# Feed-forward block sums of a hybrid diffusion step: made from kept full-precision blocks and rebuilt blocks, with no GpSimd instruction

## The chip, the core and the metric

The kernel runs on one core of a Trainium2 chip. The metric is the device time of one execution, in microseconds (us). TensorE (PE) multiplies, VectorE (DVE), ScalarE (ACT) and GpSimd (POOL) do the elementwise work, and each of them executes its own instruction stream in order. SyncE issues the weight transfers.

## The reference

Two layers run over 640 tokens (128 of a context, 512 of a latent grid) of width 1024. Each layer is a half-step SwiGLU feed-forward, a token mixer (attention in layer 0, a long convolution in layer 1), and a second feed-forward. Every sub-layer reads a modulated input and ends in a layer norm:

```
def modulate(x, shift, scale):
    return x * (1.0 + scale) + shift

def swiglu(h, w_in, w_out):
    g, u = jnp.split(h @ w_in, 2, axis=-1)
    return (jax.nn.silu(g) * u) @ w_out

x = layer_norm(ALPHA * x + 0.5 * g1 * swiglu(modulate(x, sh1, sc1), ffn_w_in_i[0], ffn_w_out_i[0]), ...)
mix, extras = mixer(modulate(x, sh2, sc2))
x = layer_norm(ALPHA * x + g2 * mix, ...)
x = layer_norm(ALPHA * x + 0.5 * g3 * swiglu(modulate(x, sh3, sc3), ffn_w_in_i[1], ffn_w_out_i[1]), ...)
```

The width of `w_in` is 2 x 2816, so each of the four feed-forwards has 22 hidden tiles of 128.

## The kernel before

Activations are stored transposed: `x[:, dt, token]` holds feature tile `dt` (0 to 7) for all 640 tokens, which fall into two halves of 320, `c = 0` and `c = 1`. Half 0 holds both kinds of tokens (128 and 192), which have different modulation vectors, so an ACT instruction that modulates a tile of half 0 is issued as two (128 and 192 columns) and one of half 1 as a single one (320 columns).

Every fp32 product is made of three reduced-precision ones: an operand is split in a high half (`xh`, `wh`, `hh`; a cast on ACT, line 157) and a low half (`xl`, `wl`, `hl`; a subtraction on DVE, line 158), and three matmuls per 128 x 128 block (lines 516 to 518) add up.

A feed-forward stage (`ffn`, `idx` 0 to 3) starts with two or three "plain" hidden tiles (`do_plain`: both gate and up product for each token half, eight feature tiles each) and makes the others "fast" (`do_fast`): a two by two block scheme with seven products of four feature tiles in place of eight. It needs sums of weight blocks, which GpSimd makes (`s1` to `s4`, lines 593 to 596, two buffers), and three sums of activation blocks, made once in each stage: with the blocks x11, x21 (half 0, feature tiles 0 to 3 and 4 to 7) and x12, x22 (half 1), T1 = x12 - x11, T2 = x22 - T1, T4 = x21 - T2, and a further one, T2 - x11, which replaces x12 in `xh` and `xl` after the plain tiles are through (`combine_rest`). `combine_blocks` makes them from the split halves `xh`, `xl` that exist already: five DVE subtractions and additions and two splits for each of four tiles, and four GpSimd instructions (lines 543 to 546), on tiles named `ta` and `tb`; the splits go to tiles named `t`.

Ahead of that stands the layer norm of half 1 (`norm_steps`), which runs beside the first plain products: when its scale `rs` is there, DVE multiplies each `x` tile by it (line 425), ACT modulates it into a temporary `xm` (line 362), and `modulate_out` splits it into `xh`, `xl`. `rescale` then turns the normalised `x` itself into its scaled form, in place, on GpSimd (line 466, 16 tiles in a stage); in program order it stands between the fast tiles. Temporaries of `tmp` share a ring of six buffers.

A plain tile's two products sit in two of five accumulator banks. The gate's bank comes free when ACT has made its Silu (line 585, tile `sg`), the up product's when DVE has multiplied it in (line 573). The order in which each engine's instructions stand is chosen at build time by a scheduler, within the dependencies; it is not written by hand.

Of the kernel before, what the change touches and what calls it, by code (L numbers as in the profile page):

```python
# [12 lines left out]
F32 = mybir.dt.float32  # L13
F32R = mybir.dt.float32r
AF = mybir.ActivationFunctionType
ALU = mybir.AluOpType
# [9 lines left out]
CH = T // 2  # L26
# [52 lines left out]
T1, T2, T4 = (0, 1), (2, 3), (4, 5)  # L79
# [5 lines left out]
def kernel(  # L85
# [5 lines left out]
    te, act, dve, pool, sp = nc.tensor, nc.scalar, nc.vector, nc.gpsimd, nc.sync  # L91
# [21 lines left out]
    def tmp(name, cols=T, parts=P, dt=F32):  # L113
        t = tp.tile([P, UW], F32, tag="t", name=name)
        return t[:parts, :cols]
# [40 lines left out]
    def split(pair, src, eng=None):  # L156
        act.copy(pair[0], src)  # L157
        (eng or dve).tensor_tensor(pair[1], src, pair[0], ALU.subtract)  # L158
# [154 lines left out]
    xh = res.tile([P, KD, T], F32R, name="xh")  # L313
    xl = res.tile([P, KD, T], F32R, name="xl")
    fill = []
    tt = []
# [19 lines left out]
    CSL = (slice(0, CH), slice(CH, T))  # L336
# [22 lines left out]
    def mod_apply(dst, dt, c, st):  # L359
        for sl, z in SEG[c]:  # L360
            o = slice(sl.start - CSL[c].start, sl.stop - CSL[c].start)
            act.activation(dst[:, o], x[:, dt, sl], AF.Identity, bias=drv[:, st, 1, dt, z:z + 1],
                           scale=drv[:, st, 0, dt, z:z + 1])

    def modulate(dt, c, st):
        modulate_out(dt, c, modulate_in(dt, c, st))

    def modulate_in(dt, c, st):
        xm = tmp(f"xm{st}_{dt}_{c}", CH)
        mod_apply(xm, dt, c, st)  # L370
        return xm

    def modulate_out(dt, c, xm):
        if dt in XDVE[c]:
            dve.tensor_copy(xh[:, dt, CSL[c]], xm)
        else:
            act.copy(xh[:, dt, CSL[c]], xm)
        eng = pool if dt in XPOOL[c] else dve
        eng.tensor_tensor(xl[:, dt, CSL[c]], xm, xh[:, dt, CSL[c]], ALU.subtract)  # L379
# [7 lines left out]
    def norm_steps(c, st, bank, nsum):  # L387
# [35 lines left out]
        for dt in range(KD + (LAG if st < 5 else 0)):  # L423
            if dt < KD:
                ins = dve.tensor_tensor(x[:, dt, sl], x[:, dt, sl], rs, ALU.mult)
                if dt > LAG:
                    pin(ins)
            if st < 5:
                if dt < KD:
                    xms.append(modulate_in(dt, c, st + 1))  # L430
                if dt >= LAG:
                    modulate_out(dt - LAG, c, xms[dt - LAG])
            else:
                act.activation(x[:, dt, sl], x[:, dt, sl], AF.Identity, bias=lnb[:, st, dt:dt + 1],
                               scale=lng[:, st, dt:dt + 1])
                sp.dma_start(out=a["y"][:, dt, sl], in_=x[:, dt, sl])
# [82 lines left out]
            if n == KD and i % 4 == 3:  # L519
                tick()  # L520

    def pair_tmp(name):
        t = tmp(name, 2 * CH)
        return t[:, 0:CH], t[:, CH:2 * CH]

    def xf(dt, c):
        return [t[:, dt, CSL[c]].bitcast(F32) for t in (xh, xl)]

    def combine_blocks(st):
        pairs = [pair_tmp(f"ta{st}_{k}") for k in range(4)]  # L530
        for k, (t1, t2) in enumerate(pairs):
            u = tmp(f"tb{st}_{k}", CH)
            (h11, l11), (h12, l12), (h22, l22) = xf(k, 0), xf(k, 1), xf(k + 4, 1)
            dve.tensor_tensor(t1, h12, h11, ALU.subtract)
            dve.tensor_tensor(u, l12, l11, ALU.subtract)
            dve.tensor_tensor(t1, t1, u, ALU.add)
            dve.tensor_tensor(t2, h22, t1, ALU.subtract)
            dve.tensor_tensor(t2, t2, l22, ALU.add)
            for src, (h, l) in ((t2, T2), (t1, T1)):
                split((tt[h][:, k], tt[l][:, k]), src)  # L540
        for k, (t1, t2) in enumerate(pairs):
            (h11, l11), (h21, l21) = xf(k, 0), xf(k + 4, 0)
            pool.tensor_tensor(t1, h21, t2, ALU.subtract)
            pool.tensor_tensor(t1, t1, l21, ALU.add)
            pool.tensor_tensor(t2, t2, h11, ALU.subtract)
            pool.tensor_tensor(t2, t2, l11, ALU.subtract)
        return pairs

    def combine_rest(pairs):
        for k, (t4, t3) in enumerate(pairs):  # L550
            split((xh[:, k, CSL[1]], xl[:, k, CSL[1]]), t3)
        for k, (t4, t3) in enumerate(pairs):
            split((tt[T4[0]][:, k], tt[T4[1]][:, k]), t4)

    def ffn(l, j, hp, fbank, following):
        idx = 2 * l + (0 if j == 0 else 1)
# [10 lines left out]
        for g0, g1 in GROUPS:  # L567
# [20 lines left out]
            def do_fast(f):  # L588
# [8 lines left out]
                for u, src in ((u11, a11), (u2, s2), (u1, s1), (u12, a12), (u3, s3), (u4, s4), (u22, a22)):  # L597
                    split(u, src)
                b1, b2, b3 = [fbank(f"f{idx}_{f}_{i}") for i in range(3)]
                p1, p5 = pair_tmp(f"p{idx}_{f}")  # L600
                q, u3_ = pair_tmp(f"q{idx}_{f}")
                sg0, sg1 = pair_tmp(f"sg{idx}_{f}")
                product(b1, [u11], 0, xb(range(4), 0))
# [18 lines left out]
            if g0 == 0:  # L622
                for f, c in [(0, 0), (1, 0), (0, 1), (1, 1)] + [(f, c) for f in range(2, NPLAIN[idx]) for c in range(2)]:
                    if (f, c) == (0, 1):
                        settle()
                        t3 = combine_blocks(st)
                    do_plain(f, c)
                combine_rest(t3)
# [417 lines left out]
    def filters(consts):  # L1046
# [8 lines left out]
        with tc.tile_pool(name="fl", bufs=1) as fl, tc.tile_pool(name="fps", bufs=3, space=PSUM) as fps, \  # L1055
# [163 lines left out]
            for it in range(8):  # L1219
                if it == XLOAD:  # L1220
                    del raws[NRAW:]
                    sp.dma_start(out=x, in_=a["xT"])
                if it == XLOAD + 1:
                    for dt in range(KD):
                        modulate(dt, 0, 0)
                gen = spectrum(it)
                for i in range(5):
                    next(gen)
                    if it + 1 < 8:
                        taps(it + 1, i)  # L1230
                    if i < SFILL[1 + it]:
                        fill_step()
                if it + 2 < 8:
                    prepare(it + 2)
# [314 lines left out]
    with es:  # L1549
        for dt in range(KD):  # L1550
            modulate(dt, 1, 0)
        ffn(0, 0, hp, fbank, [("wv", 0, 0), ("wv", 0, 1), ("wqk", 0, 0)])
# [178 lines left out]
```

## Time and profile before

| | |
|---|---|
| time, median of three runs | 2839.18 us (2838.5 to 2842.29) |
| the profiled execution's own time | 2846.74 us |
| its span, first to last instruction | 2845.0 us |
| mean granted TensorE clock, of full speed | 0.977 |
| busy: PE, DVE, ACT, POOL | 95%, 76%, 41%, 38% |

The profile is of one execution; its instructions and waits add up to the span, and some 2 us of the execution lie outside it. The median is of other executions. An engine's share is a mean over stages that have different limits.

### The profile page before, as it was taken

What the parts mean: (1) busy time and instruction counts of PE and PEld (TensorE: products, weight loads), DVE (VectorE), ACT (ScalarE), POOL (GpSimd) and SP (SyncE); (2) the same over time, 40 slices, a digit from 0 to 9 for tenths busy, and PEclk for the clock granted to TensorE, in tenths of its full rate; (3) what the DMA queues carried; (4) which work ended last, traced back from release to release, by engine and by line L of the source; (5) the groups of instructions that cost most, each with busy time, mean ns of one, the idle gap of its engine ahead of it and who ended that gap; (6) DMA issues with size and microseconds to landing.
All of it is one profiled execution on the core that took longest, in us unless ns stands there. A gap on an engine that the chain in (4) does not pass through costs nothing.

```text
span 2845.0 us, 51146 instructions
## 1 busy us (share of the span) xinstructions
PE 2702.4 (95%) x19404; PEld 2574.7 (90%) x19404; DVE 2157.5 (76%) x4778; ACT 1174.0 (41%) x2508; POOL 1067.2 (38%) x891
## 2 busy tenths in 40 slices
PE   7988999999999988999998999999999988999998
PEld 6888999989999678999988999998999987999997
DVE  6697889865665688888979888886777777865764
ACT  5642433444444353434345243344333335433433
POOL 4462543440000163534445354344223235643542
PEclk9999999999999989999999999998999999999999
DMA  8623333313222523243231433332423331212311
GB/s 289 223 69 113 118 99 119 113 54 95 76 72 73 192 68 119 90 127 123 86 105 38 130 112 108 119 111 73 130 78 109 101 97 41 90 61 89 97 62 59
DMA packets 111135, 293.46 MB, mean 103 GB/s; under 512 B 13823, under 2 KB 28927, under 8 KB 110760
## 3 DMA queue, kind: packets, MB, share of 16 engines
q1 hardware_dynamic: 107576, 285.80, 31.4%
q0 software_dynamic: 2304, 4.20, 0.5%
q8 instruction: 153, 2.51, 0.4%
q14 instruction: 94, 0.77, 0.1%
q10 hardware_dynamic: 1008, 0.19, 0.1%
HBM read 275.98 MB, written 14.16 MB: 102 GB/s over the span
## 4 chain that ended last, share of the span: by engine, by line
PE 62%; DVE 21%; DMA 6%; issue 4%; POOL 4%; ACT 3%; DVEq 0%; SPq 0%; POOLq 0%; ACTq 0%
PE f L516 6%; PE f L517 6%; PE f L518 6%; PE o L516 5%; PE o L517 5%; PE o L518 5%; DVE junk L247 4%; DVE wl L158 4%; DMA mh<-in_modt 3%; DVE xl L158 2%; PE hy L343 2%; PE hy L342 2%; PE hy L344 2%; POOL s L595 2%; POOL s L596 2%
## 5 line engine op out<-in xcount | busy, mean ns | idle before, releaser
L157 ACT CAST wh<-raw 128x512 fp32r<-128x512 f32 (+1 forms) x327 | 230.3, 709 | 302.5 <-PE o L517 150.7
L158 DVE TENSOR_TENSOR wl<-raw,wh 128x512 fp32r<-128x512 f32 (+1 forms) x274 | 280.5, 1025 | 72.3 <-ACT wh L157 71.3
L516 PE MATMUL f<-xh,wh 128*128 128x320 f32 x956 | 302.3, 319 | 25.6 <-DVE q L606 13.5
L517 PE MATMUL f<-xl,wh 128*128 128x320 f32 x956 | 301.6, 316 | 3.2 <-DVE xl L379 3.1
L518 PE MATMUL f<-xh,wl 128*128 128x320 f32 x956 | 298.1, 314 | 0.0
L247 DVE SCALAR_TENSOR_TENSOR junk<-mh,condw 128x256 f32<-128x256 f32 x576 | 267.4, 511 | 34.1 <-DMA mh<-in_modt 33.8
L516 PE MATMUL o<-hh,wh 128*128 128x320 f32 x840 | 260.7, 314 | 5.2 <-ACT hh L157 5.2
L517 PE MATMUL o<-hl,wh 128*128 128x320 f32 x840 | 259.0, 309 | 0.0
L518 PE MATMUL o<-hh,wl 128*128 128x320 f32 x840 | 258.1, 309 | 0.0
L353 DVE SCALAR_TENSOR_TENSOR x<-o,drv,x 128x320 f32<-128x320 f32 (+2 forms) x384 | 153.8, 434 | 102.6 <-PE o L518 102.2
L158 DVE TENSOR_TENSOR wl<-s,wh 128x512 fp32r<-128x512 f32 x187 | 172.4, 922 | 72.0 <-ACT wh L157 68.5
L157 ACT CAST wh<-s 128x512 fp32r<-128x512 f32 x187 | 115.7, 620 | 242.6 <-POOL s L594 73.7
L516 PEld LDWEIGHTS f<-xh,wh 128*128 128x128 f32 x956 | 183.8, 193 | 31.8 <-DVE q L606 16.0
L516 PE MATMUL f<-xh,xh 128*128 128x320 f32 x628 | 196.6, 315 | 11.7 <-DVE q L606 5.3
L595 POOL TENSOR_TENSOR s<-raw,raw 128x512 f32<-128x512 f32 x77 | 115.9, 1506 | 238.1 <-DVE wl L158 149.9
L593 POOL TENSOR_TENSOR s<-raw 128x512 f32<-128x512 f32 x77 | 110.7, 1437 | 248.7 <-DVE junk L247 167.5
L517 PE MATMUL f<-xl,xh 128*128 128x320 f32 x628 | 195.5, 312 | 0.2 <-DVE xl L379 0.2
L518 PE MATMUL f<-xh,xl 128*128 128x320 f32 x628 | 193.8, 311 | 0.0
L517 PEld LDWEIGHTS f<-xl,wh 128*128 128x128 f32 x956 | 184.5, 193 | 6.1 <-DVE xl L379 5.8
L518 PEld LDWEIGHTS f<-xh,wl 128*128 128x128 f32 x956 | 183.8, 193 | 0.0
L516 PE MATMUL o<-hh,xh 128*128 128x320 f32 x568 | 177.7, 315 | 3.6 <-ACT hh L157 3.6
L517 PE MATMUL f<-t,wh 128*128 128x320 f32 x560 | 173.6, 311 | 4.1 <-DVE t L158 4.1
(490 smaller groups left out, 8975.5 us busy)
## 6 DMA issues: line engine op xcount, KB each, us to landing
raw<-in_win SPq DMA_DIRECT2D x176, 512.0 KB, 3.6
raw<-in_wout SPq DMA_DIRECT2D x88, 512.0 KB, 4.3
mh<-in_modt SPq DMA_DIRECT2D x144, 256.0 KB, 2.9
raw<-in_modw SPq DMA_DIRECT2D x62, 512.0 KB, 4.9
raw<-in_hyin SPq DMA_DIRECT2D x24, 512.0 KB, 4.0
ksb<-kspec SPq DMA_DIRECT2D x40, 256.0 KB, 2.7
kspec<-ks SPq DMA_DIRECT2D x32, 256.0 KB, 3.2
raw<-in_wqk SPq DMA_DIRECT2D x16, 512.0 KB, 3.7
```

Source lines behind the costliest of these rows:

```text
L157: act.copy(pair[0], src)
L158: (eng or dve).tensor_tensor(pair[1], src, pair[0], ALU.subtract)
L247: dve.scalar_tensor_tensor(junk, raw[:, 256 * g:256 * g + 256], 1.0, condw[0][:, z], ALU.mult, ALU.mult, accum_out=acc[:, g0 + g, t, z:z + 1])
L342: te.matmul(ps, wh[:, i, cols], kh(k), start=(i == 0), stop=False)
L343: te.matmul(ps, wh[:, i, cols], kl(k), start=False, stop=False)
L344: te.matmul(ps, wl[:, i, cols], kh(k), start=False, stop=(i == n - 1))
L353: dve.scalar_tensor_tensor(x[:, dt, sl], ps[:, o], drv[:, st, 2, dt, z:z + 1], x[:, dt, sl], ALU.mult, ALU.add)
L516: te.matmul(ps, wh, kh, start=(first and i == 0), stop=False, skip_group_check=True)
L517: te.matmul(ps, wh, kl, start=False, stop=False, skip_group_check=True)
L518: te.matmul(ps, wl, kh, start=False, stop=(last and i == n - 1), skip_group_check=True)
L593: pool.tensor_tensor(s1, a21, a22, ALU.add)
L595: pool.tensor_tensor(s3, a11, a21, ALU.subtract)
```

## The change

`modulate_in` keeps the full-precision modulated tiles of half 1 in feed-forward stages: two of them share one buffer of the ring (`kept_xm`, tiles `xk`), so that four buffers hold all eight. `combine_blocks` takes x12 and x22 from there, and rebuilds x11 and x21 by modulating `x` of half 0 again with ScalarE (tile `tb`, two tiles of two instructions each). The sums are made from these with four DVE subtractions and three splits for each of four tiles, and none on GpSimd. The fourth sum is written into buffers of kept tiles that are no longer needed, so that two of the four buffers come free. `rescale` of half 0 may no longer overwrite `x` before the rebuilding has read it.

```
@@ modulate_in
+    kept_xm = {}
+
+    def pair_tmp(name):
+        t = tmp(name, 2 * CH)
+        return t[:, 0:CH], t[:, CH:2 * CH]
...
     def modulate_in(dt, c, st):
-        xm = tmp(f"xm{st}_{dt}_{c}", CH)
+        if c == 1 and st % 3 != 1:
+            if dt < 4:
+                kept_xm[dt] = pair_tmp(f"xk{st}_{dt}")
+            xm = kept_xm[dt % 4][dt // 4]
+        else:
+            xm = tmp(f"xm{st}_{dt}_{c}", CH)
         mod_apply(xm, dt, c, st)
         return xm
@@ combine_blocks, combine_rest
     def combine_blocks(st):
-        pairs = [pair_tmp(f"ta{st}_{k}") for k in range(4)]
+        pairs, thirds = [kept_xm.pop(k) for k in range(4)], []
         for k, (t1, t2) in enumerate(pairs):
-            u = tmp(f"tb{st}_{k}", CH)
-            (h11, l11), (h12, l12), (h22, l22) = xf(k, 0), xf(k, 1), xf(k + 4, 1)
-            dve.tensor_tensor(t1, h12, h11, ALU.subtract)
-            dve.tensor_tensor(u, l12, l11, ALU.subtract)
-            dve.tensor_tensor(t1, t1, u, ALU.add)
-            dve.tensor_tensor(t2, h22, t1, ALU.subtract)
-            dve.tensor_tensor(t2, t2, l22, ALU.add)
-            for src, (h, l) in ((t2, T2), (t1, T1)):
-                split((tt[h][:, k], tt[l][:, k]), src)
-        for k, (t1, t2) in enumerate(pairs):
-            (h11, l11), (h21, l21) = xf(k, 0), xf(k + 4, 0)
-            pool.tensor_tensor(t1, h21, t2, ALU.subtract)
-            pool.tensor_tensor(t1, t1, l21, ALU.add)
-            pool.tensor_tensor(t2, t2, h11, ALU.subtract)
-            pool.tensor_tensor(t2, t2, l11, ALU.subtract)
-        return pairs
-
-    def combine_rest(pairs):
-        for k, (t4, t3) in enumerate(pairs):
+            x11, x21 = pair_tmp(f"tb{st}_{k}")
+            mod_apply(x11, k, 0, st)
+            mod_apply(x21, k + 4, 0, st)
+            dve.tensor_tensor(t1, t1, x11, ALU.subtract)
+            dve.tensor_tensor(t2, t2, t1, ALU.subtract)
+            split((tt[T2[0]][:, k], tt[T2[1]][:, k]), t2)
+            split((tt[T1[0]][:, k], tt[T1[1]][:, k]), t1)
+            dve.tensor_tensor(x21, x21, t2, ALU.subtract)
+            t3 = pairs[k - k % 2][1 - k % 2]
+            dve.tensor_tensor(t3, t2, x11, ALU.subtract)
+            thirds.append(t3)
+            split((tt[T4[0]][:, k], tt[T4[1]][:, k]), x21)
+        return thirds
+
+    def combine_rest(thirds):
+        for k, t3 in enumerate(thirds):
             split((xh[:, k, CSL[1]], xl[:, k, CSL[1]]), t3)
-        for k, (t4, t3) in enumerate(pairs):
-            split((tt[T4[0]][:, k], tt[T4[1]][:, k]), t4)
```

The scheduler's order moves with it, in much the same way in the second, third and fourth feed-forward. Three places of the second one follow (lines behind the edit are numbered one less, those between the two edits 11 more). First GpSimd, from the layer norm's subtractions (`x<-x,mus`) to the sums of the second fast tile. Before:

```order
L466 TENSOR_SCALAR x<-x,lng,lnb 128x320 x6
L400 TENSOR_TENSOR x<-x,mus_1_11626 128x320 x3
L466 TENSOR_SCALAR x<-x,lng,lnb 128x320 x8
L595 TENSOR_TENSOR s_3_2_12144<-raw_98,raw_99 128x512
L543 TENSOR_TENSOR ta_0_11834<-xh,ta_0_11834 128x320
L544 TENSOR_TENSOR ta_0_11834<-ta_0_11834,xl 128x320
L596 TENSOR_TENSOR s_3_3_12145<-raw_98,s_3_1_12143 128x512
L545 TENSOR_TENSOR ta_0_11834<-ta_0_11834,xh 128x320
L546 TENSOR_TENSOR ta_0_11834<-ta_0_11834,xl 128x320
L593 TENSOR_TENSOR s_4_0_12277<-raw_101 128x512
```

And now:

```order
L411 TENSOR_TENSOR x<-x,mus_1_11614 128x320 x3
L477 TENSOR_SCALAR x<-x,lng,lnb 128x320 x12
L594 TENSOR_TENSOR s_3_2_12120<-raw_98,raw_99 128x512
L477 TENSOR_SCALAR x<-x,lng,lnb 128x320
L595 TENSOR_TENSOR s_3_3_12121<-raw_98,s_3_1_12119 128x512
L477 TENSOR_SCALAR x<-x,lng,lnb 128x320 x3
L592 TENSOR_TENSOR s_4_0_12253<-raw_101 128x512
```

The `ta` instructions are gone, all rescales stand behind the layer norm's subtractions, and the weight sum `s_3_2` stands behind twelve of them.

Second ScalarE, from the cast of that weight sum (`wh_104<-s_3_2`) to the Silu of the first plain tile of half 1 (`sg_0_1`). Before:

```order
L157 CAST wh_104<-s_3_2_12144 128x512
L157 CAST xh_1_11262<-raw_101 128x512
L157 CAST xh_1_11266<-s_3_1_12143 128x512
L157 CAST t_1_11276<-ta_0_11834 128x320
L157 CAST wh_102<-raw_98 128x512
L157 CAST t_1_11274<-ta_1_11835 128x320
L157 CAST t_1_11274<-ta_2_11836 128x320
L585 ACTIVATE sg_0_1_11944<-f_0_1_0_11894 128x320
```

And now:

```order
L157 CAST wh_104<-s_3_2_12120 128x512
L362 ACTIVATE tb_2_11848<-x,drv 128x128
L362 ACTIVATE tb_2_11848<-x,drv 128x192
L362 ACTIVATE tb_2_11848<-x,drv 128x128
L362 ACTIVATE tb_2_11848<-x,drv 128x192
L362 ACTIVATE tb_3_11863<-x,drv 128x128
L362 ACTIVATE tb_3_11863<-x,drv 128x192
L362 ACTIVATE tb_3_11863<-x,drv 128x128
L362 ACTIVATE tb_3_11863<-x,drv 128x192
L157 CAST t_1_11262<-xk_2_11754 128x320
L157 CAST xh_1_11250<-raw_101 128x512
L584 ACTIVATE sg_0_1_11928<-f_0_1_0_11878 128x320
```

Between that cast and the Silu stand the eight instructions that rebuild the third and fourth pair of blocks, where three casts of sums and three of weights stood.

Third VectorE, around the split of the last feature tile of half 1 (`xl<-xm_7_1`, now the upper half of the kept buffer `xk_3`). Before:

```order
L379 TENSOR_TENSOR xl<-xm_6_1_11786,xh 128x320
L534 TENSOR_TENSOR ta_1_11835<-xh 128x320
L573 TENSOR_TENSOR sg_1_0_11829<-sg_1_0_11829,f_1_0_1_11804 128x320
L379 TENSOR_TENSOR xl<-xm_7_1_11791,xh 128x320
L537 TENSOR_TENSOR ta_0_11834<-xh,ta_0_11834 128x320
L535 TENSOR_TENSOR tb_1_11848<-xl 128x320
```

And now:

```order
L545 TENSOR_TENSOR xk_0_11748<-xk_1_11751,tb_1_11833 128x320
L158 TENSOR_TENSOR xl_1_11253<-raw_98,xh_1_11252 128x512
L158 TENSOR_TENSOR wl_103<-s_3_0_12118,wh_102 128x512
L158 TENSOR_TENSOR t_1_11265<-xk_0_11748,t_1_11264 128x320
L158 TENSOR_TENSOR t_1_11263<-xk_1_11751,t_1_11262 128x320
L158 TENSOR_TENSOR t_1_11267<-tb_0_11818,t_1_11266 128x320
L158 TENSOR_TENSOR t_1_11265<-xk_1_11751,t_1_11264 128x320
L158 TENSOR_TENSOR t_1_11267<-tb_1_11833,t_1_11266 128x320
L545 TENSOR_TENSOR xk_0_11748<-xk_0_11748,tb_0_11818 128x320
L390 TENSOR_TENSOR xl<-xk_3_11759,xh 128x320
```

The sums of the first two pairs are now complete ahead of that split. From the first multiplication by `rs` up to it there are 37 VectorE instructions, where there were 25; from the start of the stage to the last split of a sum there are four fewer. TensorE does the same 144 matmuls between `rs` and the third plain tile's second product as before; those that need the last feature tile of half 1 now stand last among them.

## Rows read from the trace of the kernel before

**Rows 1.** The page: busy time of each engine.

```profile
PE 2702.4 (95%) x19404; PEld 2574.7 (90%) x19404; DVE 2157.5 (76%) x4778; ACT 1174.0 (41%) x2508; POOL 1067.2 (38%) x891
```

**Rows 2.** Busy us (instructions) of PE, PEld, DVE, ACT, POOL; clock; DMA: four stretches.

```profile
129.00:187.00 58.00, 50.65 (x327) 49.81 (x326) 52.49 (x79) 31.30 (x66) 34.57 (x26) 0.94 0.21 64
1024.00:1091.00 67.00, 58.80 (x368) 57.59 (x367) 62.30 (x97) 34.15 (x73) 43.91 (x35) 0.92 0.13 40
1501.00:1592.00 91.00, 80.69 (x510) 79.15 (x510) 86.43 (x160) 43.32 (x91) 52.06 (x43) 0.94 0.28 85
2391.00:2450.00 59.00, 51.79 (x324) 50.33 (x323) 55.39 (x86) 29.37 (x63) 39.29 (x33) 0.94 0.14 45
```

**Rows 3.** PE's waits over the whole span: us in total, times, longest.

```profile
PE f L517 <- DVE t L158: 13.7, 5, 5.4
PE f L516 <- DVE sg L573: 9.4, 3, 4.2
...
PE f L516 <- ACT sg L585: 1.7, 2, 0.9
```

**Rows 4.** PE's waits for `q` in the second, third and fourth stretch of rows 2.

```profile
PE f L516 <- DVE q L606: 2.7, 1, 2.7
...
PE f L516 <- DVE q L606: 2.9, 2, 1.9
...
PE f L516 <- DVE q L606: 1.0, 1, 1.0
```

**Rows 5.** POOL's groups: one of four `ta` lines (1000 to 1090 us); weight sum (page).

```profile
L544 POOL TENSOR_TENSOR ta<-ta,xl 128x320 f32<-128x320 f32 x4 | 4.8, 1190 | 0.1
...
L595 POOL TENSOR_TENSOR s<-raw,raw 128x512 f32<-128x512 f32 x77 | 115.9, 1506 | 238.1 <-DVE wl L158 149.9 <-DVE xl L158 87.7
```

**Rows 6.** DVE in order of time, second feed-forward: start, us, line, operation.

```profile
1024.77 1.28 DVE L425 TENSOR_TENSOR x<-x,rs 128x320 f32<-128x320 f32 x3
...
1029.06 0.72 DVE L379 TENSOR_TENSOR xl<-xm,xh 128x320 fp32r<-128x320 f32 x1
...
1036.48 0.48 DVE L379 TENSOR_TENSOR xl<-xm,xh 128x320 fp32r<-128x320 f32 x1
...
1053.93 0.47 DVE L573 TENSOR_TENSOR sg<-sg,f 128x320 f32<-128x320 f32 x1
...
1056.81 1.15 DVE L537 TENSOR_TENSOR ta<-xh,ta 128x320 f32<-128x320 f32 x1
```

**Rows 7.** POOL in order of time, the same feed-forward.

```profile
1028.83 0.61 POOL L466 TENSOR_SCALAR x<-x,lng,lnb 128x320 f32<-128x320 f32 x1 [0.67 <-ACT xm L362]
...
1038.52 4.23 POOL L595 TENSOR_TENSOR s<-raw,raw 128x512 f32<-128x512 f32 x1 [3.10 <-DVE wl L158]
...
1056.50 1.11 POOL L544 TENSOR_TENSOR ta<-ta,xl 128x320 f32<-128x320 f32 x1
```

**Rows 8.** DVE's largest group of `combine`, 1020 to 1080 us.

```profile
L158 DVE TENSOR_TENSOR t<-ta,t 128x320 fp32r<-128x320 f32 x12 | 10.9, 908 | 0.0
```

**Rows 9.** ACT's groups by shape, 1000 to 1090 us.

```profile
L362 ACT ACTIVATE xm<-x,drv 128x192 f32<-128x192 f32 x8 | 4.3, 532 | 0.0
L362 ACT ACTIVATE xm<-x,drv 128x128 f32<-128x128 f32 x8 | 3.9, 487 | 4.3 <-DVE x L425 4.3
```

**Rows 10.** ACT in order of time, the same feed-forward.

```profile
1009.58 1.75 ACT L362 ACTIVATE xm<-x,drv 128x128 f32<-128x128 f32 x4 [1.23 <-DVE x L425]
...
1042.78 0.62 ACT L157 CAST wh<-s 128x512 fp32r<-128x512 f32 x1 [5.72 <-POOL s L595]
...
1045.95 0.43 ACT L585 ACTIVATE sg<-f 128x320 f32<-128x320 f32 x1
```

**Rows 11.** PE in order of time, the same feed-forward.

```profile
1024.14 0.56 PE L516 MATMUL f<-xh,wh 128*128 128x320 f32 x1
...
1045.35 0.31 PE L518 MATMUL f<-xh,wl 128*128 128x320 f32 x1
1046.43 0.42 PE L516 MATMUL f<-xh,xh 128*128 128x320 f32 x1 [0.77 <-ACT sg L585]
```

More of the change, by code (lines that the diff above doesn't have):

```diff
@@ L520, in product @@
                 tick()
[L522 to L527, printed above, removed]
     def combine_blocks(st):
-        pairs = [pair_tmp(f"ta{st}_{k}") for k in range(4)]
+        pairs, thirds = [kept_xm.pop(k) for k in range(4)], []
         for k, (t1, t2) in enumerate(pairs):
-            u = tmp(f"tb{st}_{k}", CH)
-            (h11, l11), (h12, l12), (h22, l22) = xf(k, 0), xf(k, 1), xf(k + 4, 1)
-            dve.tensor_tensor(t1, h12, h11, ALU.subtract)
-            dve.tensor_tensor(u, l12, l11, ALU.subtract)
-            dve.tensor_tensor(t1, t1, u, ALU.add)
-            dve.tensor_tensor(t2, h22, t1, ALU.subtract)
-            dve.tensor_tensor(t2, t2, l22, ALU.add)
-            for src, (h, l) in ((t2, T2), (t1, T1)):
-                split((tt[h][:, k], tt[l][:, k]), src)
-        for k, (t1, t2) in enumerate(pairs):
-            (h11, l11), (h21, l21) = xf(k, 0), xf(k + 4, 0)
-            pool.tensor_tensor(t1, h21, t2, ALU.subtract)
-            pool.tensor_tensor(t1, t1, l21, ALU.add)
-            pool.tensor_tensor(t2, t2, h11, ALU.subtract)
-            pool.tensor_tensor(t2, t2, l11, ALU.subtract)
-        return pairs
-    def combine_rest(pairs):
-        for k, (t4, t3) in enumerate(pairs):
+            x11, x21 = pair_tmp(f"tb{st}_{k}")
[13 more added lines that the diff above has]
+        for k, t3 in enumerate(thirds):
             split((xh[:, k, CSL[1]], xl[:, k, CSL[1]]), t3)
-        for k, (t4, t3) in enumerate(pairs):
-            split((tt[T4[0]][:, k], tt[T4[1]][:, k]), t4)
     def ffn(l, j, hp, fbank, following):
```

## The prediction

> **What bounds the kernel now.** I read the page first. TensorE is busy 95% of the span [rows 1], so what can be won without fewer matmuls is the time in which it waits, or runs at the lower of its two clocks. Then I looked for the four places at which the edited code works, one in each feed-forward, and asked for busy time and clock there [rows 2]. Two things are to be seen. VectorE, 76% busy over the span, is busy for 52.5 of 58, 62.3 of 67, 86.4 of 91 and 55.4 of 59 us: here it has almost no slack, while ScalarE is about half busy. And the mean granted clock is 0.92 to 0.94, where 1 is 2.4 GHz and 0.5 is 1.2 GHz: half-rate stretches cost 0.06 x 58 + 0.08 x 67 + 0.06 x 91 + 0.06 x 59 = 17.9 us.
>
> The list of waits says what TensorE waits for. For the low half of an activation sum (`t`): 13.7 us in 5 waits; for the multiplication behind Silu, which frees a plain tile's accumulator bank: 9.4 us in 3; for the Silu of such a tile: 1.7 us in 2 [rows 3]. These arise in the four places alone. For `q`, the first VectorE instruction on a fast tile's products, it waits in many places; in the three later ones it is 2.7 + 2.9 + 1.0 = 6.6 us [rows 4]. Together 31.4 us idle and 17.9 us of clock, 49.3 us: more than that the change can't win. The clock costs 17.9 / 31.4 = 0.57 us per idle us here, and I use that ratio below for idle time added or removed.
>
> **Removed.** Sixteen GpSimd instructions in each feed-forward, of about 1.15 us each (1.19 in one of the four groups [rows 5], 1.11 for one of them [rows 7]), some 18 us. GpSimd itself does not bound anything: it is busy 34.6 of 58 us and less than three quarters in all four places [rows 2]. What matters is what they do to VectorE. A subtraction of 320 columns takes 0.48 us alone (1036.48) and 1.15 us (1056.81) beside such an instruction, which ran from 1056.50 to 1057.61 [rows 6, 7]. The twelve low halves of sums in the second feed-forward took 0.908 us on average [rows 8]: 12 x 0.43 = 5.1 us lost in this group alone. If every one of the sixteen delayed one VectorE instruction by 0.67 us, it would be 10.7 us in a feed-forward. The relief is between 5.1 and 10.7 us, and I take 9, near the upper end, since the group of rows 8 is a third of the edited VectorE work and bears about half. Besides, four VectorE instructions fewer are issued in each feed-forward, at 0.40 us from start to start (three in 1.28 us, 1024.77 [rows 6]): 1.6 us. So VectorE gets back about 10.6 us in each place, where TensorE waits 31.4 / 4 = 7.9 us on average.
>
> **Added.** Sixteen ScalarE instructions in each feed-forward, half of 128 columns (0.487 us) and half of 192 (0.532 us) [rows 9], in sequence about 0.42 us apart (four in 1.75 us [rows 10]): 16 x 0.42 = 6.7 us, at most 16 x 0.51 = 8.2. In the second place ScalarE is busy 34.2 of 67 us [rows 2], so there is room for it on average. It is free where nothing waits behind it; that is so in the first feed-forward, where half 0 and half 1 are modulated ahead of the plain tiles, and not in the other three.
>
> **Moved.** In these three the sums of the first two pairs are now ahead of the split of half 1's last feature tile, which came at 1036.48 [rows 6]. There are 12 more VectorE instructions up to it, so 12 x 0.40 = 5 us: 1041.5, and up to 1044.5 where rescales delay twelve of them by 0.24 us each (below). TensorE has work for that time: from 1024.14, when `rs` is out, to 1045.35 it does 144 matmuls without that tile's being missed [rows 11], and the same 144 stand there after the change, with those that need the last tile put last. So this split is just in time: 0 to 1 us of waiting.
>
> Then the next block needs the bank of the first plain tile of half 1, and with it the Silu. Now the Silu starts at 1045.95, and TensorE waits 0.77 us for it [rows 10, 11]. After the change it stands behind the cast of the weight sum `s_3_2`, eight rebuilding instructions and two casts: 8 x 0.42 + 0.43 (320 columns) + 0.62 (512 columns) = 4.4 us behind that cast [rows 10]. The cast waits for GpSimd, as it does now for 5.72 us [rows 10]: GpSimd made that sum in 4.23 us from 1038.52 [rows 7], nearly three times its line's mean of 1.506 [rows 5]. The buffer for it is free when the split of `s_3_0` is through, which has 7 VectorE instructions between it and the last split, thus 1039 to 1042, and the sum takes 1.5 to 4.2 us. The cast then starts at 1040.5 to 1046.2, the Silu ends 0.62 + 4.4 + 0.43 us later, at 1046 to 1051.7, and TensorE, ready at 1045.7, waits 0.3 to 6 us; for the lower end I keep 1 us, with what the last split may add. I take 3.5 us, the middle of 1 and 6, in each of three feed-forwards. It stands in place of the 0.77 us and of most of the wait for the multiplication, since that one (1053.93 now [rows 6]) comes only ten VectorE instructions, 4 to 5 us, behind the last split, and a product of 24 matmuls (21.2 / 144 = 0.147 us each, 3.5 us) lies between.
>
> The rescales that GpSimd does with the normalised `x` now stand beside the sums. The nearest row: one ran at 1028.83, and the split beside it took 0.72 us where 0.48 is usual [rows 6, 7], so 0.24 us each at most, against 0.67 for a `ta` instruction. I charge it in the 1044.5 above and not again.
>
> **The sum**, in idle us. Gone: waits for `t` 13.7, for the multiplication 9.4, for the Silu 1.7, half of those for `q` 3.3 (VectorE is ahead of its work by more than they are long, but part of them come later in the fast tiles, from weight splits); 28.1. New: 3 x 3.5 = 10.5. Net 17.6, with the clock at 0.57 each 27.6 us. The profiled execution took 2846.7 us and would take 2819.1; it lies 7.5 us above the median of the runs, so for the median 2839.2 - 27.6 = 2811.6: **2812 us**. Its own range: with 1 us of new waiting and all of `q` gone (31.4 - 3) x 1.57 = 44.6 us, 2795; with 6 us and none of `q` gone (24.8 - 18) x 1.57 = 10.7 us, 2829.
>
> **Rivals.** *The rescales take the place of what is removed.* Sixteen in each of the three later feed-forwards come to lie beside VectorE's sums (the first has none). If each held a two-input VectorE instruction as a `ta` one does, 16 x 0.67 = 10.7 us would be put back there, and only the 1.6 us of fewer instructions remain. The first place keeps its gain, at most about the longest wait for `t`, 5.4 x 1.57 = 8.5 us [rows 3]; the Silu's new place takes 3 x (3.5 - 0.8) x 1.57 = 12.7. So 2839.2 - 3 x 1.6 - 8.5 + 12.7 = 2838.6: no change. For it: they read the same memory at the same time. Against it: 0.24, not 0.67, in the row above. The Trainium skill ("SBUF — State Buffer", Who interferes with whom) says that a VectorE instruction with two SBUF inputs contends with any GpSimd instruction that reads SBUF; for the `ta` instructions the trace agrees (0.48 to 1.15 us), and for rescales, which read SBUF too, it shows a third of it. By that sentence alone this rival would be the forecast.
>
> *ScalarE's queue becomes the bound (slower).* One mechanism: the cast of `s_3_2` waits for GpSimd, which gets nothing done beside an unbroken VectorE, and eight rebuilding instructions and the Silu stand behind it, while TensorE has all five banks full. With a wait of S us in three feed-forwards the time changes by (3 S - 24.8) x 1.57; it is slower than before from S = 8.3 us, and by 17.6 us (2857) at S = 12. That needs the Silu at 1057 and the sum more than 10 us late. Against it: VectorE's own next split needs that cast, so it pauses and lets GpSimd through.
>
> *All of it goes,* since ScalarE reaches the Silu in time: 2795, the end worked out above. That the change would not do what it says I leave out: the instruction counts of the built program show 64 fewer on GpSimd, 16 fewer on VectorE and 64 more on ScalarE.
>
> **Numbers.** Forecast 0.64 (2800 to 2829); all gone 0.12; rescales in their place, no change, 0.13; slower 0.11. A change of 0.2%, 5.7 us, is about what a measurement of this kernel can tell from none. So faster 0.76, same 0.13, slower 0.11. The range of 8 in 10 leaves out the slower case and half of the best one, and takes in no change: 2796 to 2840; the faster cases alone lie in 2795 to 2829.
>
> **What would show it.** Right: no wait of TensorE for `t` left, or under 3 us of the 13.7; low halves of sums near 0.5 us in place of 0.908; clock 0.96 or more in the first place; one new wait of 1 to 6 us for the Silu (line 584) in each of the three others; the last split of half 1 at 5 to 8 us behind its old place. Wrong: VectorE subtractions of 0.7 us and more beside rescales; waits for the Silu of more than 8 us, or for the last splits of half 1; waits for `q` as long as before in spite of an idle VectorE.

## The result, and the profile after

| | before | after |
|---|---|---|
| time, median of 4 runs each, same chip | 2838.84 us (2834.42 to 2842.29) | 2797.55 us (2794.62 to 2810.63) |
| ratio, 95% interval | 1 | 0.9861 (0.9844 to 0.9879) |
| the profiled execution: span | 2845.0 us | 2795.6 us |
| mean granted TensorE clock | 0.977 | 0.986 |

The kernel became 41 us faster. The forecast was 2812 us with a range of 2796 to 2840; the result lies in it, near the case in which all the waits go. The page's first line, after:

```profile
PE 2680.6 (96%) x19404; PEld 2557.1 (91%) x19404; DVE 2103.9 (75%) x4762; ACT 1196.1 (43%) x2572; POOL 1005.4 (36%) x827
```

To compare the four places, I took in the trace after the stretches between the same two matmuls, by their number, as in [rows 2]. Busy us (instructions) of PE, PEld, DVE, ACT and POOL, the clock, and DMA:

```profile
132.66:187.49 54.83, 49.42 (x328) 48.89 (x326) 44.91 (x81) 38.71 (x85) 20.19 (x11) 0.97 0.23 73
1013.16:1069.71 56.55, 54.38 (x367) 53.72 (x366) 50.74 (x92) 39.17 (x89) 33.95 (x27) 1.00 0.16 48
1479.18:1560.17 80.99, 76.93 (x510) 76.00 (x509) 73.83 (x165) 48.62 (x107) 45.06 (x35) 0.98 0.32 99
2350.54:2400.77 50.23, 48.05 (x324) 47.31 (x323) 45.03 (x85) 35.52 (x81) 31.22 (x25) 1.00 0.18 53
```

The same work took 58 + 67 + 91 + 59 = 275.0 us before [rows 2] and takes 242.6 now, 32.4 less. TensorE's busy time in it fell from 241.9 to 228.8 us for the same matmuls, which is the clock (0.92 to 0.94 before, 0.97 to 1.00 now), and its idle time from 33.1 to 13.8 us. VectorE's fell from 256.6 to 214.5 us; it had almost no slack, and now has 5 to 10 us in each place. A further 7.2 us were won right behind the first place, in the first fast tiles of the first feed-forward. Before, from 187 to 300 us:

```profile
187.00:300.00 113.00, 102.30 (x674) 99.17 (x673) 92.23 (x230) 35.68 (x71) 43.99 (x32) 0.95 0.35 105
```

and after, the same matmuls:

```profile
187.49:293.24 105.75, 99.15 (x674) 97.04 (x673) 85.94 (x224) 34.03 (x68) 42.39 (x30) 0.98 0.34 110
```

TensorE's waits over the whole span, after, against [rows 3, 4] (us in total, times, longest):

```profile
PE f L527 <- DVE q L605: 11.2, 10, 3.5
PE f L527 <- ACT sg L584: 11.0, 4, 5.1
```

The 13.7 us for `t` and the 9.4 us for the multiplication behind Silu are gone from this list (one wait of 0.33 us for `t` is left). What has come is 11.0 us for the Silu in four places. VectorE's low halves of sums, 1020 to 1080 us, against [rows 8]:

```profile
L158 DVE TENSOR_TENSOR t<-xk,t 128x320 fp32r<-128x320 f32 x8 | 4.8, 614 | 0.0
L158 DVE TENSOR_TENSOR t<-tb,t 128x320 fp32r<-128x320 f32 x4 | 1.9, 478 | 0.0
```

Twelve took 10.9 us, now 6.7 us. The new waits for the Silu, first by TensorE, in the first and in the second feed-forward:

```profile
172.35 0.64 PE L527 MATMUL f<-xh,wh 128*128 128x320 f32 x1 [5.08 <-ACT sg L584]
...
1036.77 0.42 PE L527 MATMUL f<-xh,xh 128*128 128x320 f32 x1 [2.00 <-ACT sg L584]
```

ScalarE at the same two places (start, us, line, operation, idle time before it and what ended it):

```profile
170.82 0.62 ACT L157 CAST xh<-s 128x512 fp32r<-128x512 f32 x1 [5.08 <-POOL s L593]
171.35 0.61 ACT L157 CAST xh<-raw 128x512 fp32r<-128x512 f32 x1
171.87 0.43 ACT L584 ACTIVATE sg<-f 128x320 f32<-128x320 f32 x1
...
1030.95 0.62 ACT L157 CAST wh<-s 128x512 fp32r<-128x512 f32 x1 [1.85 <-POOL s L594]
1032.10 3.41 ACT L362 ACTIVATE tb<-x,drv 128x128 f32<-128x128 f32 x8 [0.53 <-DVE t L158]
...
1036.29 0.43 ACT L584 ACTIVATE sg<-f 128x320 f32<-128x320 f32 x1
```

and GpSimd, whose weight sums the two casts waited for:

```profile
164.18 6.61 POOL L593 TENSOR_TENSOR s<-s,raw 128x512 f32<-128x512 f32 x1 [4.11 <-DVE wl L158]
...
1029.52 1.40 POOL L594 TENSOR_TENSOR s<-raw,raw 128x512 f32<-128x512 f32 x1 [0.68 <-DVE wl L158]
```

In the second feed-forward the queue is the one foretold: the cast of the weight sum, eight rebuilding instructions, the Silu. In the first one nothing is rebuilt between the two; there GpSimd took 6.61 us for one sum, and the Silu stood behind the cast that needed it.

### The profile page after: what moved, and what is told of

The parts are those of the page before. It is cut to its first block, busy times and chain, and to the rows that moved or that the text cites. A ratio compares the mean times of both kernels' runs of the same rounds, so it can differ in the third digit from the quotient of the medians.

```text
span 2795.6 us, 51136 instructions
## 1 busy us (share of the span) xinstructions
PE 2680.6 (96%) x19404; PEld 2557.1 (91%) x19404; DVE 2103.9 (75%) x4762; ACT 1196.1 (43%) x2572; POOL 1005.4 (36%) x827
## 4 chain that ended last, share of the span: by engine, by line
PE 64%; DVE 20%; DMA 6%; issue 4%; ACT 3%; POOL 3%; SPq 0%; DVEq 0%; ACTq 0%; POOLq 0%
PE f L527 7%; PE f L528 7%; PE f L529 7%; PE o L527 5%; PE o L528 5%; PE o L529 5%; DVE junk L247 5%; DVE wl L158 3%; DMA mh<-in_modt 3%; DVE xl L158 2%; PE hy L343 2%; PE hy L342 2%; PE hy L344 2%; POOL s L595 2%; PE qk L342 1%
## 5 line engine op out<-in xcount | busy, mean ns | idle before, releaser
L158 DVE TENSOR_TENSOR wl<-raw,wh 128x512 fp32r<-128x512 f32 (+1 forms) x274 | 270.5, 989 | 74.1 <-ACT wh L157 72.8
```

## The experiments

Two questions were open. Is the gain the relief from contention, or the new way of making the sums? And what holds the new Silu waits? All kernels were timed in five rounds against the kernel before on the same chip. "Against after" is the difference of the two ratios times 2840 us; since each ratio is known to about 0.0015, differences under some 6 us say nothing. The times in the expectations go with a kernel before of 2838.8 us; on the other chips it took 2841.9 to 2842.9 us, so they are compared by this column. "Four places" is the time of the same matmuls as above, in one profile. The scheduler orders each kernel anew, so an edit also moves some instructions that it doesn't name; where that bears on a reading it is said.

| kernel | median us | ratio (95%) | against after, us | four places, us |
|---|---|---|---|---|
| before | 2838.8 to 2842.9 | 1 | +39 | 274.9 |
| after | 2797.55 | 0.9861 (0.9844 to 0.9879) | 0 | 242.6 |
| sums on VectorE | 2803.28 | 0.9862 (0.9845 to 0.9878) | 0 | 243.8 |
| the same, own `sg` buffer | 2802.04 | 0.9860 (0.9846 to 0.9874) | 0 | 244.1 |
| late second half of the sums | 2802.29 | 0.9859 (0.9845 to 0.9872) | -1 | 239.0 |
| without rescales | 2804.1 | 0.9871 (0.9853 to 0.9888) | +3 | 246.4 |
| after, own `sg` buffer | 2808.67 | 0.9878 (0.9864 to 0.9892) | +5 | 251.5 |
| two subtractions on GpSimd | 2808.92 | 0.9888 (0.9871 to 0.9905) | +8 | 253.7 |
| no rebuilding, own `sg` buffer | 2817.64 | 0.9912 (0.9898 to 0.9926) | +14 | 255.8 |
| 64 one-input GpSimd added | 2818.54 | 0.9915 (0.9901 to 0.9928) | +15 | 260.7 |
| 64 VectorE added | 2823.22 | 0.9933 (0.9918 to 0.9949) | +20 | 256.3 |
| 64 GpSimd one-column reads with two fills each added | 2824.76 | 0.9946 (0.9929 to 0.9964) | +24 | 261.2 |
| 64 two-input GpSimd added | 2832.2 | 0.9965 (0.9952 to 0.9978) | +30 | 278.0 |
| no rebuilding | 2836.95 | 0.9984 (0.9974 to 0.9994) | +35 | 271.6 |

**Sums on VectorE.** The kernel before, with one edit, which takes GpSimd out of the sums and changes nothing else in the source:

```
-            pool.tensor_tensor(t1, h21, t2, ALU.subtract)
-            pool.tensor_tensor(t1, t1, l21, ALU.add)
...
+            dve.tensor_tensor(t1, h21, t2, ALU.subtract)
+            dve.tensor_tensor(t1, t1, l21, ALU.add)
...
```

> The kernel before, with its sixteen GpSimd instructions of the sums in each feed-forward moved to VectorE and nothing else changed: no rebuilding, no kept tiles, no contention from `ta`. VectorE gets 16 x 0.40 = 6.4 us more to do in each feed-forward and is relieved of up to 10.7 us of contention. Contention theory: faster than before by 5 to 25 us, 2814 to 2834 us. Rival (the number of VectorE instructions decides, since VectorE bounds these places): slower than before by 4 x 6.4 x 1.57 = 40 us at most, 2850 to 2880 us.

The page's first line:

```profile
PE 2682.7 (96%) x19404; PEld 2555.0 (91%) x19404; DVE 2141.8 (76%) x4842; ACT 1173.0 (42%) x2508; POOL 1005.9 (36%) x827
```

It has the whole gain, more than the contention theory allowed (39 us, where 5 to 25 were expected): 80 VectorE instructions more than the changed kernel and no rebuilding, and the same time. So the gain needs nothing of the change but that GpSimd is out of the sums; kept tiles and rebuilding together bring nothing that can be measured.

**The traffic put back.** Sixteen instructions a feed-forward are added to the changed kernel, of three kinds on GpSimd and of one on VectorE; they write a scratch tile (`junks`) that nobody reads. Two-input:

```
             split((tt[T4[0]][:, k], tt[T4[1]][:, k]), x21)
+            for _ in range(4):
+                pool.tensor_tensor(junks[-1], tt[T2[1]][:, k].bitcast(F32), tt[T1[1]][:, k].bitcast(F32), ALU.subtract)
```

> The changed kernel with sixteen more GpSimd instructions in each feed-forward: two-input subtractions of 320 columns that read the low halves of two finished sums and write a scratch tile that nobody reads. They put the traffic of the removed `ta` instructions back beside VectorE without anybody waiting for their results. Theory (the old `ta` instructions cost by contention): VectorE instructions beside them take 0.9 to 1.15 us again, and 15 to 35 us of the gain of 41 are lost: 2812 to 2833 us. Rival (the gain came from fewer VectorE instructions and from sums that no longer wait for GpSimd): within 6 us of the changed kernel, 2797 to 2803 us.

One-input, `pool.tensor_scalar(junks[-1], tt[T2[1]][:, k].bitcast(F32), lng[:, 0, 0:1], lnb[:, 0, 0:1], ALU.mult, ALU.add)` in its place:

> As the run with sixteen two-input GpSimd instructions, but with one-input ones (multiply and add with two columns, the form of the rescales) at the same places. Theory (a rescale costs VectorE 0.24 us, a `ta` instruction 0.67): about a third of the loss of the two-input run, 3 to 12 us over the changed kernel, 2800 to 2810 us. Rival (a rescale holds VectorE as long as a `ta` instruction): the same loss as in the two-input run, and VectorE instructions of 0.9 us and more beside them.

Fills, two behind each read of one column, which fixes the place:

```
+            for _ in range(4):
+                pool.tensor_scalar(junks[-1][:, 0:1], tt[T2[1]][:, k, 0:1].bitcast(F32), ...)
+                for _ in range(2):
+                    pool.memset(junks[-1], 0.0)
```

> The changed kernel with sixteen additions on GpSimd in each feed-forward that keep it busy for some 0.8 us each and read almost nothing: one column of a finished sum (which fixes the place) and two fills of a 320-column scratch tile. Theory (all that a further GpSimd instruction costs is its contention with VectorE): VectorE instructions beside the fills keep 0.48 us, and the time is that of the changed kernel, 2794 to 2801 us. Rival (a part is that the weight sums stand behind them in GpSimd's queue and come later): VectorE unhindered as well, but 5 to 12 us over the changed kernel, 2802 to 2810 us, with VectorE and ScalarE waiting longer for weight sums.

And the two-input form with `dve` for `pool`:

> As the run with sixteen two-input subtractions into a scratch tile on GpSimd (2832 us), but the same sixteen on VectorE. Theory (on VectorE each takes 0.40 us from start to start, on GpSimd it delays VectorE by 0.59 us): 64 x 0.40 = 26 us of VectorE work, of which a half to three quarters shows, 2810 to 2818 us, less than on GpSimd. Rival (once the contention is gone VectorE has room, as 80 instructions more made no difference in the kernel with all sums on VectorE): 2795 to 2804 us. Second rival (an instruction costs the same on either engine): 2828 us and more.

The matmuls of the second place took 56.55 us in the changed kernel, with VectorE busy for 50.74 of them (above). With two-input GpSimd instructions:

```profile
1016.36:1083.13 66.77, 57.97 (x367) 56.73 (x366) 63.35 (x92) 39.54 (x90) 48.91 (x43) 0.95 0.13 40
```

With one-input ones:

```profile
1010.70:1073.52 62.82, 57.95 (x368) 56.43 (x367) 54.23 (x92) 39.16 (x89) 49.14 (x43) 0.95 0.15 43
```

With fills:

```profile
1016.15:1079.25 63.10, 56.57 (x367) 55.25 (x366) 49.98 (x92) 38.34 (x88) 53.49 (x75) 0.97 0.14 43
```

With the sixteen on VectorE:

```profile
1018.97:1077.90 58.93, 55.13 (x367) 53.73 (x366) 57.02 (x106) 38.40 (x86) 36.24 (x26) 1.00 0.14 45
```

In the first three VectorE executes the same 92 instructions, in 63.35, 54.23 and 49.98 us. The order is nearly that of the changed kernel too: without the added ones GpSimd's instructions stand as they did there, and 27, 8 and 15 of VectorE's 4762 stand elsewhere. So there are two prices. Two-input instructions hold VectorE: the page has it busy for 2151.9 us against 2103.9 with as many instructions, 48.0 us for 64. The groups of VectorE that were at 614 and 478 ns, in that run, 1010 to 1085 us:

```profile
L158 DVE TENSOR_TENSOR t<-xk,t 128x320 fp32r<-128x320 f32 x8 | 6.2, 789 | 0.0
L158 DVE TENSOR_TENSOR t<-tb,t 128x320 fp32r<-128x320 f32 x4 | 4.8, 1200 | 0.0
```

The loss of 30 us lies in the theory's 15 to 35. Fills don't hold VectorE at all (2103.7 us busy), and cost 24 us nevertheless, twice what the rival expected: the theory that contention is all is refuted. What they delay is the weight sum behind them in GpSimd's queue. ScalarE's waits for the third of the four weight sums, in the run with fills (us in total, times, longest):

```profile
ACT wh L157 <- POOL s L601: 46.8, 39, 5.7
ACT xh L157 <- POOL s L601: 44.2, 29, 5.7
```

and in the changed kernel, where that sum is line 594:

```profile
ACT wh L157 <- POOL s L594: 37.4, 40, 2.2
...
ACT xh L157 <- POOL s L594: 26.1, 28, 2.2
```

Over all four sums and both kinds of cast these waits add up to 306.0 us in the changed kernel, 342.6 with fills, 337.0 with one-input and 306.5 with two-input instructions.

How both prices reach TensorE is to be seen behind ScalarE's copy `p` of a fast tile's product, for which TensorE doesn't wait in the four places of the changed kernel. With fills it waits 10.8 us there, and each time the copy stands behind a cast that waited for a weight sum:

```profile
1061.96 0.62 ACT L157 CAST xh<-s 128x512 fp32r<-128x512 f32 x1 [5.66 <-POOL s L601]
1062.49 0.42 ACT L614 COPY p<-f 128x320 f32<-128x320 f32 x1
1062.96 0.46 PE L530 MATMUL f<-xh,wh 128*128 128x320 f32 x1 [2.82 <-ACT p L614]
```

With two-input instructions it waits 11.0 us there, and each time the copy stands behind a cast that waited for a multiplication of VectorE, which had no idle time:

```profile
1063.91 0.46 ACT L157 CAST hh<-sg 128x320 fp32r<-128x320 f32 x1 [3.75 <-DVE sg L577]
...
1064.80 0.42 ACT L608 COPY p<-f 128x320 f32<-128x320 f32 x1
1065.27 0.63 PE L530 MATMUL f<-xh,wh 128*128 128x320 f32 x1 [3.74 <-ACT p L608]
```

So the fills pay by the queue, the two-input ones by contention, and the one-input ones (12.0 us more on VectorE, 15 us of time, half the two-input loss where a third was expected) mostly by the queue. Each read of one column took GpSimd 1.5 us with its two fills, not the expected 0.8 (16 reads 12.6 us, 32 fills 11.7 in the second place), more than a one-input instruction (1.08 us); that fits the higher cost. The Trainium skill ("SBUF — State Buffer", Who interferes with whom) says that VectorE's two-input instructions contend with GpSimd instructions that read SBUF and not with those that only write it. For the fills the trace agrees (-0.2 us on VectorE); for one-input reads the hold was a quarter of that of two-input ones (12.0 and 48.0 us).

On VectorE itself the sixteen cost 20 us and not 30. Expected were 13 to 21 over the changed kernel, so the theory holds, and the rival that VectorE has room to spare does not. The 0.59 us by which the expectation lets a GpSimd instruction delay VectorE came out as 0.75. The 80 further instructions of "sums on VectorE" are then likely paid by something that it saves; what it lacks is the rebuilding, but that this is what pays is argued, not shown.

**Two subtractions on GpSimd.**

```
-            dve.tensor_tensor(x21, x21, t2, ALU.subtract)
+            pool.tensor_tensor(x21, x21, t2, ALU.subtract)
...
-            dve.tensor_tensor(t3, t2, x11, ALU.subtract)
+            pool.tensor_tensor(t3, t2, x11, ALU.subtract)
```

> The changed kernel with two of its four subtractions per tile (the fourth sum and T2 - x11) on GpSimd: eight GpSimd instructions in each feed-forward, whose results are used, and eight VectorE instructions fewer. Theory (cost by the number of two-input GpSimd instructions, about 30 us for 64 of them): 10 to 18 us over the changed kernel, 2807 to 2816 us. Rival (what costs is that somebody waits for GpSimd's result): over 25 us, 2822 us and more. Second rival (eight VectorE instructions fewer outweigh it): 2790 to 2800 us.

It cost 8 us, just under the 10 to 18 expected from the number alone and far under the 25 of the rival; that somebody waits for GpSimd's result is not what costs most. VectorE had 32 instructions less to do, so the price of GpSimd's 32 alone isn't measured.

**Late second half of the sums.** The sums of pairs three and four are issued behind the first plain tile of half 1:

```
...
+                        combine_blocks(st, (0, 1), pairs, t3)
                     do_plain(f, c)
+                    if (f, c) == (0, 1):
+                        combine_blocks(st, (2, 3), pairs, t3)
```

> The changed kernel with the sums of the third and fourth pair, and their eight rebuilding instructions, issued behind the first plain tile of half 1 and not ahead of it, so that its Silu doesn't stand behind them on ScalarE. Theory (the Silu waits of 11.0 us in four places are caused by what stands ahead in ScalarE's queue): TensorE's waits for the Silu fall to under 3 us and the time by 8 to 17 us, to 2780 to 2790 us. Rival (VectorE is the bound there, and the wait only changes its name, to the multiplication behind Silu, to `t` or to `q`): 2793 to 2802 us, with new waits of 8 us and more.

TensorE's waits in it:

```profile
PE f L527 <- DVE q L604: 17.9, 12, 3.6
...
PE f L527 <- ACT sg L583: 5.2, 3, 1.7
```

The Silu waits fell from 11.0 to 5.2 us, not under the 3 of the theory, those for `q` rose from 11.2 to 17.9, by 6.7 and not the rival's 8, and the time stayed. In time the rival was right: what is put off is missed by the first fast tiles.

**No rebuilding.** Half 1 from the kept tiles, half 0 from `xh` and `xl`, all on VectorE:

```
...
-            mod_apply(x11, k, 0, st)
-            mod_apply(x21, k + 4, 0, st)
-            dve.tensor_tensor(t1, t1, x11, ALU.subtract)
...
+            dve.tensor_tensor(t1, t1, h11, ALU.subtract)
+            dve.tensor_tensor(t1, t1, l11, ALU.subtract)
...
```

> The changed kernel without the rebuilding: half 1 still from the kept full-precision tiles, half 0 from its split halves `xh`, `xl`, everything on VectorE. Sixteen ScalarE instructions fewer and twelve VectorE instructions more in each feed-forward than in the changed kernel, and four fewer on VectorE than in the kernel before with its GpSimd instructions moved to VectorE. Theory (the Silu waits of 11.0 us are the price of the rebuilding on ScalarE, and VectorE has room once the contention is gone): 2780 to 2791 us. Rival (what the rebuilding costs is won by its fewer VectorE instructions; as long as GpSimd is kept out, all ways of making the sums end alike): 2793 to 2806 us.

Both were wrong: nearly all of the gain is lost, without a GpSimd instruction in the sums. (VectorE has 32 instructions less than in "sums on VectorE", eight a feed-forward and not the four of the expectation.) TensorE's first wait in the list:

```profile
PE f L527 <- ACT sg L589: 36.1, 4, 10.4
```

and ScalarE where it was waited for in the second feed-forward:

```profile
1042.19 0.61 ACT L157 CAST wh<-s 128x512 fp32r<-128x512 f32 x1
1046.32 0.44 ACT L589 ACTIVATE sg<-f 128x320 f32<-128x320 f32 x1 [3.52 <-DVE t L158]
```

VectorE, just ahead of that:

```profile
1045.81 0.48 DVE L158 TENSOR_TENSOR t<-tb,t 128x320 fp32r<-128x320 f32 x1
```

The Silu doesn't need the split `t<-tb` that released it for its data; it writes `sg`, which takes a buffer of the ring of six, and that split is the last to read one. So I gave `sg` of the plain tiles one buffer of its own, here and in two other kernels. In all three the scheduler also moved the first Silus, and ScalarE loads its function table 21 times in place of 15 (1.28 us each), so they change a little more than the buffer:

```
-                sg = tmp(f"sg{idx}_{f}_{c}", CH)
+                sg = hp.tile([P, CH], F32, tag="sg", name=f"sg{idx}_{f}_{c}", bufs=1)
```

In "no rebuilding":

> The kernel with kept half 1, half 0 from its split halves and no rebuilding, which waited 36.1 us for four Silus, but with the Silu tile `sg` of the plain tiles in one buffer of its own and not in the ring of six that the sums use. Theory (the Silu waits for a buffer of the ring, which a VectorE split of the fourth sums frees late): waits for the Silu under 10 us and 25 to 50 us off its 2837 us, 2787 to 2812 us. Rival (the Silu is late because of the casts ahead of it in ScalarE's queue): 2825 to 2840 us, and waits of over 25 us.

TensorE's waits for the Silu there:

```profile
PE f L527 <- ACT sg L589: 13.3, 6, 3.2
```

The ring was the larger part: 22.8 us of waits and 20 us of time gone, less than the 25 expected, with 13.3 us of waits left. Three of the six waits left, 3.2 us each, stand behind a cast that waited 4.7 us for GpSimd's third weight sum. What else keeps this kernel 14 us behind "sums on VectorE", with 32 VectorE instructions fewer, stays open. In the changed kernel:

> The changed kernel with the Silu tile `sg` of the plain tiles in one buffer of its own. Theory (in the changed kernel these waits of 11.0 us come from ScalarE's queue, a cast that waits for GpSimd and the rebuilding, not from the ring): 2794 to 2802 us, waits for the Silu of 8 us or more. Rival (the ring of six buffers causes them here too): waits under 4 us, 2780 to 2791 us.

12.3 us of Silu waits stayed and nothing was won, so there the ring is not the cause (5 us against after are within the uncertainty). And in "sums on VectorE":

> The kernel before with its GpSimd instructions of the sums on VectorE, and the Silu tile `sg` of the plain tiles in one buffer of its own. It had hardly a wait for the Silu (2803 us). Theory (the ring costs nothing there): 2798 to 2808 us. Rival (the multiplication and the first rests on the ring as well): 2785 to 2797 us, which would beat the changed kernel.

No difference, as expected: the ring costs nothing there.

**Without rescales.** The 48 rescales of three feed-forwards are left out (the call of `rescale` in the fast tiles is replaced by `pass`), so `x` keeps its unscaled form.

> The changed kernel without the 48 rescales of the normalised `x` in the feed-forwards (they are left out, so `x` keeps its unscaled form). Theory (a rescale costs VectorE 0.24 us and GpSimd's queue some 0.9 us): 4 to 12 us faster than the changed kernel, 2785 to 2794 us. Rival of the prediction (each holds VectorE like a `ta` instruction, 16 x 0.67 us in each of three places): 30 us and more, below 2770 us. Second rival (hidden wholly): 2794 to 2801 us.

VectorE was busy 11.5 us less over the span, 0.24 us for each rescale, and the time stayed within its uncertainty. They are hidden; the rival is out.

No kernel was measurably faster than the changed one.

## Why the prediction was right, and where not

**The bound.** Right. The waits listed in the prediction and the clock in the four places held 32.4 of the gain, and the first feed-forward's fast tiles, which I had left out of the first place, 7.2. The other 9.8 of the 49.4 us between the two profiles are spread over the rest of the span; the profiled execution of before lay 7.5 us above its median.

**The net idle time** was forecast at 17.6 us less, and fell by 19.3 in the four places. Of its parts the waits for `t` and for the multiplication went as foretold. Of those for `q`, where half of 6.6 was counted, all went from the three places, and 2.4 us came back just behind the second; over the span they lost 7.6.

**The clock** was the term that was too small: 0.57 us for each idle us gave 10.0 us; the busy time for the same matmuls fell by 13.1. By the prediction's own formula the half-rate stretches cost 17.8 us before (not 17.9) and 3.3 now: the granted clock rose to 1.00 in two places, and four fifths of the loss went, not a share in proportion to the idle time (19.3 of 33.1). These 3.1 us, 1.7 of idle time and 7.2 in the fast tiles make 12.0; the forecast of 27.6 was short by 12 us by the ratio and by 14 by the medians.

**The new wait.** 3 x 3.5 = 10.5 us was forecast, and 11.0 measured, but that the two agree is luck. Behind the rebuilding it is 2.00, 1.95 and 1.99 us, 5.9 in all, in the forecast range of 0.3 to 6 and under the value taken; the weight sum took 1.40 us, just under the 1.5 to 4.2 that I gave. The step that failed is that the sum has no new wait in the first feed-forward: 5.08 us there, by the very mechanism that I gave the slower rival (GpSimd gets little done beside an unbroken VectorE). The sum that had begun at 164.18 ended at 170.79 us, just behind the first pause of VectorE (last section).

**The last split of half 1** came 19.0 us behind the first multiplication by `rs` (1013.81 to 1032.80) in place of 11.7 [rows 6], 7.3 us later; forecast were 5 to 8, and no wait. The waits of TensorE for such splits are 1.9 us over the span.

**Removed contention.** Right in size: VectorE's busy time in the four places fell by 42.1 us, 10.5 in each, where 9 and 1.6 were forecast, and the run with 64 two-input instructions put 48.0 us back on VectorE and lost 30 of the 39. But "GpSimd itself does not bound anything" was too strong. A busy share of less than three quarters hides that ScalarE's casts wait for weight sums in GpSimd's queue; in the run with fills that costs 24 us. How much of the gain of the change itself came by this second way, and how much by VectorE, was not separated. That ScalarE's waits for weight sums, 323.4 us before, are still 306.0 in the changed kernel and 315.9 in "sums on VectorE" speaks for a small part.

**Fewer VectorE instructions and the rebuilding**, which the prediction booked as 1.6 us a place won and as a small price, cancel: without both ("sums on VectorE") the time is the same. Why exactly they do is argued, not shown.

**The rivals.** *Rescales:* out, nothing won without them. Splits beside them take 0.72 us, which the prediction had named as a sign of being wrong (0.7 and more); that line was badly drawn, since they took 0.72 before [rows 6], and the price of 0.24 us each is what was measured. *ScalarE's queue:* the waits stayed at 2 to 5 us; "no rebuilding" shows what happens at 10.36 us in three places, though by a buffer and not by the queue: by the rival's formula it would be 10 us slower than before, and it came out 4.5 us faster.

## What to carry to other kernels

Price a helper engine's instruction twice: by what it does to VectorE beside it (0.75 us for each two-input one here), and by what stands behind it in its own queue; the engine's busy share shows neither. Before rewriting an algorithm to take work off GpSimd, try the one-word edit that puts the same instructions on the busy engine: here it had the whole gain. When an instruction is released by one whose data it doesn't use, look for the buffer that it writes.

## What the runs showed of the hardware

GpSimd can be held up by VectorE, not slowed in proportion: a 512-column sum that takes 1.3 to 1.5 us ran for 6.61 us beside unbroken two-input instructions of VectorE and ended 1.1 us after these paused. VectorE in the changed kernel, in order of time:

```profile
168.18 0.68 DVE L158 TENSOR_TENSOR xl<-s,xh 128x512 fp32r<-128x512 f32 x1
168.79 0.88 DVE L158 TENSOR_TENSOR xl<-xk,xh 128x320 fp32r<-128x320 f32 x2
171.47 1.21 DVE L158 TENSOR_TENSOR xl<-s,xh 128x512 fp32r<-128x512 f32 x1 [1.81 <-ACT xh L157]
```

The two xl ended at 169.67 us and GpSimd's sum at 170.79; the pause itself was a wait for the cast of that sum, so the hold-up ended when VectorE ran out of work that didn't need GpSimd. The sum of 4.23 us in the kernel before [rows 7] ended likewise 1.2 us after VectorE's last instruction ahead of a pause. Which of the two is held up differs: at 157.45 us in the changed kernel a VectorE subtraction that takes 0.48 us alone took 1.47 beside such a sum, which took its usual 1.48.

In the run with fills the length hardly matters, and VectorE beside it does. GpSimd, in order of time:

```profile
1054.96 1.46 POOL L552 TENSOR_SCALAR junk<-t,lng,lnb 128x1 f32<-128x1 f32 x1
...
1057.37 0.34 POOL L552 TENSOR_SCALAR junk<-t,lng,lnb 128x1 f32<-128x1 f32 x1
1057.77 0.79 POOL L554 MEMSET junk<- 128x320 f32 x2
```

and VectorE:

```profile
1056.90 0.48 DVE L612 TENSOR_TENSOR q<-f,p 128x320 f32<-128x320 f32 x1
1062.61 0.69 DVE L158 TENSOR_TENSOR xl<-s,xh 128x512 fp32r<-128x512 f32 x1 [5.24 <-ACT xh L157]
```

The reads of a single column took 0.34 us wherever VectorE was idle (22 of the 64), and 1.10 us on average, up to 1.62, beside its instructions. The fills of 320 columns took 0.36 us in both cases and did not touch VectorE.
